# Row maxima that ignore NaN: the tiles from 53 on divided anew, shared ScalarE steps, and rows without a number found in two steps instead of three

## The chip, the cores and the metric

The kernel runs on one core of a Trainium2 chip. The time is the device time of one execution in microseconds (us). It was measured in several rounds in which the kernel before and the kernel under test ran on the same chip. The span in a profile is about 1.8 us shorter than the time of the same execution.

## The reference

```python
batch, seq, dim = 32, 2048, 2048
x = np.random.randn(batch, seq, dim).astype(np.float32)
x[np.random.rand(batch, seq, dim) < 0.1] = np.nan
np.nanmax(x, axis=-1).astype(np.float32)
```

65,536 rows of 2048 numbers, 537 MB, give 65,536 maxima. Every tenth number is a NaN and must be ignored. A row of NaN alone must give NaN. No such row occurs in the data, so the path for it was executed but never put to a test.

## The kernel before

Each of the 128 partitions takes 512 rows. They come in 74 tiles, most of 28 quarter-rows (7 rows, 7.34 MB over all partitions), into three buffers in turn. A tile is described by three lists in quarter-rows: its loads, the pieces in which it is cleaned, and its reductions.

```python
    + [([28], [7, 9, 12], [16, 12])] * 12
    + [([15, 13], [12, 12, -4], [12, 8, 8])]
    ...
    + [([4, 4, 4, 3, 5, 4, 4], [4, 4, 4, -3, 2, 3, 4, 4], [4, 4, 4, 4, 4, 4, 4])]
    + [([3, 5, 4, 1, 3, 3, 3, 2, 2, 1, 1], [-2, 1, 2, 3, 4, -1, 3, 3, -1, 2, 2, 2, -2], [4, 4, 4, 4, 4, 2, 2, 4])]
GROUPS = [TILES[:14]] + [TILES[i : i + 12] for i in range(14, 62, 12)] + [TILES[62:72], TILES[72:]]
FLAGGED = (4, 5, 6)
```

A piece passes three engines. ScalarE (ACT) turns the upper halves of its numbers into keys in which a NaN is the smallest. GpSimd (POOL), or ScalarE itself for a piece with a minus sign, turns the keys back and writes them over the numbers. VectorE (DVE) then reduces whole rows with max.

```python
e = act(here + kold, out=kp, in_=xp.bitcast(i16)[:, 1::2], func=ACT.Prelu, ...)
if back:
    e = act([e], out=xp.bitcast(i16)[:, 1::2], in_=kp, func=ACT.Copy, ...)
else:
    e = pool([e], out=xp.bitcast(i16)[:, 1::2], in0=kp, scalar1=-1.0, ...)
...
e = dve([e for a, b, e in clean if b > lo and a < done] + part, nc.vector.tensor_reduce, out=to, ...)
```

After each group named in FLAGGED, two VectorE instructions, called a step below, go over the maxima that no earlier step has gone over: one marks rows without a number, the other turns them to NaN. There are three such steps: the first, the middle and the last. The maxima of each group are stored at the end, behind all loads. A load waits for its buffer, which the last reduction of the tile three earlier frees.

## Time and profile before

| | before |
|---|---|
| time | 1254.44 us (1254.4 to 1254.58, 3 runs) |
| span in the profile | 1252.5 us |
| busy | GpSimd 93%, VectorE 89%, ScalarE 79% |
| landing of a whole tile | every 16.91 us (434 GB/s) |
| last load lands | 1242.8 us |
| last VectorE instruction ends | 1249.84 us |
| last store, 7 KB, issue to landing | 1.40 us |

The last store in the view of DMA issues (size of one, then us from issue to landing):

```profile
out_dram<-acc SPq DMA_DIRECT2D x1, 7.0 KB, 1.4
```

### The profile page before, as it was taken

What the parts mean: (1) busy time and instruction counts of PE and PEld (TensorE: products, weight loads), DVE (VectorE), ACT (ScalarE), POOL (GpSimd) and SP (SyncE); (2) the same over time, 40 slices, a digit from 0 to 9 for tenths busy, and PEclk for the clock granted to TensorE, in tenths of its full rate; (3) what the DMA queues carried; (4) which work ended last, traced back from release to release, by engine and by line L of the source; (5) the groups of instructions that cost most, each with busy time, mean ns of one, the idle gap of its engine ahead of it and who ended that gap; (6) DMA issues with size and microseconds to landing.
All of it is one profiled execution on the core that took longest, in us unless ns stands there. A gap on an engine that the chain in (4) does not pass through costs nothing.

```text
span 1252.5 us, 882 instructions
## 1 busy us (share of the span) xinstructions
DVE 1110.9 (89%) x180; ACT 987.4 (79%) x273; POOL 1168.2 (93%) x237
## 2 busy tenths in 40 slices
DVE  0888989888889988898988888898888899999999
ACT  3777887778787877788777877887777878889997
POOL 2999989998999899998999899989999999999997
DMA  9999999999999999999999999999999999999996
GB/s 414 440 418 432 440 440 440 434 416 440 440 440 436 414 440 440 438 436 425 430 440 440 438 434 418 440 440 438 436 419 436 440 426 436 429 430 434 430 427 279
DMA packets 16712, 537.20 MB, mean 429 GB/s; under 512 B 2753, under 2 KB 2753, under 8 KB 4161
## 3 DMA queue, kind: packets, MB, share of 16 engines
q1 hardware_dynamic: 16704, 537.14, 99.3%
q14 instruction: 8, 0.06, 0.0%
HBM read 536.87 MB, written 0.26 MB: 429 GB/s over the span
## 4 chain that ended last, share of the span: by engine, by line
DMA 36%; DVE 32%; POOL 21%; ACT 10%; issue 1%; SPq 0%
DMA xt<-in_x_dram 36%; DVE acc L183 32%; POOL xt L179 21%; ACT kt L175 9%; ACT xt L175 1%; DVE xt L183 0%; DVE none L183 0%; SPq L217 0%; SPq L370 0%; SPq L171 0%
## 5 line engine op out<-in xcount | busy, mean ns | idle before, releaser
L179 POOL TENSOR_SCALAR xt<-kt 128x4608 int16<-128x4608 uint16 (+10 forms) x233 | 1168.0, 5013 | 77.2 <-ACT kt L175 58.6
L183 DVE TENSOR_REDUCE acc<-xt 128x3 f32<-128x6144 f32 (+4 forms) x172 | 1107.7, 6491 | 137.7 <-POOL xt L179 128.1
L175 ACT ACTIVATE kt<-xt,scalars 128x3584 uint16<-128x3584 int16 (+8 forms) x252 | 936.8, 3755 | 256.8 <-DMA xt<-in_x_dram 233.7
L175 ACT ACTIVATE xt<-kt 128x3584 int16<-128x3584 uint16 (+5 forms) x19 | 51.2, 2697 | 0.6
L175 ACT ACT_TABLE_LOAD x1 | 1.3, 1283 | 0.9 <-SPq L171 0.9
L183 DVE TENSOR_REDUCE xt<-xt 128x1 f32<-128x1024 f32 x1 | 1.2, 1217 | 0.0
L183 DVE TENSOR_SCALAR none<-acc 128x428 int32<-128x428 f32 (+2 forms) x3 | 1.0, 339 | 0.1
L183 DVE TENSOR_TENSOR acc<-acc,none 128x428 int32<-128x428 int32 (+2 forms) x3 | 1.0, 333 | 0.1
L185 DVE MEMSET scalars<- 128x1 f32 x1 | 0.1, 59 | 1.0 <-SPq L171 1.0
L356 POOL MEMSET const-float32-0.0<- 128x1 f32 x1 | 0.1, 99 | 0.2 <-issue 0.2
L175 ACT ACTIVATE scalars<-scalars 128x1 f32<-128x1 f32 x1 | 0.2, 203 | 0.0
L356 POOL MEMSET const-bfloat16-1.0<- 128x1 bf16 x1 | 0.1, 103 | 0.0
L356 POOL MEMSET const-uint8-127<- 128x1 uint8 x1 | 0.1, 103 | 0.0
L356 POOL MEMSET const-float32-1.0<- 128x1 f32 x1 | 0.1, 99 | 0.0
## 6 DMA issues: line engine op xcount, KB each, us to landing
xt<-in_x_dram SPq DMA_DIRECT2D x60, 7168.0 KB, 22.5
xt<-in_x_dram SPq DMA_DIRECT2D x3, 3840.0 KB, 14.7
xt<-in_x_dram SPq DMA_DIRECT2D x3, 3328.0 KB, 22.2
xt<-in_x_dram SPq DMA_DIRECT2D x8, 1024.0 KB, 26.5
xt<-in_x_dram SPq DMA_DIRECT2D x2, 4096.0 KB, 21.8
xt<-in_x_dram SPq DMA_DIRECT2D x2, 3584.0 KB, 20.0
xt<-in_x_dram SPq DMA_DIRECT2D x2, 3072.0 KB, 20.6
xt<-in_x_dram SPq DMA_DIRECT2D x3, 2048.0 KB, 30.3
```

The lines of the kernel that those rows point to most:

```text
L175: return order.add("act", nc.scalar, lambda: nc.scalar.activation(**kw), deps)
L179: "pool", nc.gpsimd, lambda: nc.gpsimd.tensor_scalar(**kw), deps
L183: return order.add("dve", nc.vector, lambda: do(**kw), deps)
L185: e_top = order.add("dve", nc.vector, lambda: nc.vector.memset(top, EDGE), [])
L356: nc = _bacc.Bacc("TRN2", target_bir_lowering=False, num_devices=1)
```

## The change

The intent is to bring VectorE's end nearer to the last landing. Three things change: the tiles from 53 on are divided differently, with fewer reductions (164 for 173); neighbouring pieces may share one ScalarE key step (a tuple in the list); and groups and steps are placed so that the first step over the maxima falls before the last fourteen tiles and the second at the very end.

```diff
-    + [([28], [7, 9, 12], [16, 12])] * 12
-    + [([15, 13], [12, 12, -4], [12, 8, 8])]
...
+    + [([19, 9], [12, (5, -7), 4], [12, 16])]
...
+    + [([6, 5, 4, 5, 4, 4], [6, 5, (-3, 1), 3, 2, 4, (-2, 2)], [4, 8, 8, 8])]
+    + [([5, 4, 4, 4, 3, 4, 4], [2, 3, 4, (1, -2), 2, 3, 3, 4, (-1, 3)], [4, 8, 4, 4, 4, 4])]
+    + [([4, 4, 3, 2, 3, 4, 1, 2, 3, 2], [4, 4, 3, -2, 3, (3, -1), 3, (-1, 1), 2, -1], [4, 4, 4, 4, 4, 4, 4])]
...
-GROUPS = [TILES[:14]] + [TILES[i : i + 12] for i in range(14, 62, 12)] + [TILES[62:72], TILES[72:]]
-FLAGGED = (4, 5, 6)
+GROUPS = [TILES[i : i + 15] for i in range(0, 60, 15)] + [TILES[60:]]
+FLAGGED = (3, 4)
...
-                for c in pieces:
-                    back, c = c < 0, abs(c) * Q
+                for parts in pieces:
+                    parts = parts if isinstance(parts, tuple) else (parts,)
+                    c = sum(map(abs, parts)) * Q
...
+                    for c in parts:
+                        back, c = c < 0, abs(c) * Q
```

## The prediction

> **What bounds the kernel now.** I read the page's DMA rows first, because a kernel that reads 537 MB and writes almost nothing may have nothing else to gain.
>
> ```profile
> DVE 1110.9 (89%) x180; ACT 987.4 (79%) x273; POOL 1168.2 (93%) x237
> ...
> DMA  9999999999999999999999999999999999999996
> GB/s 414 440 418 432 440 440 440 434 416 440 440 440 436 414 440 440 438 436 425 430 440 440 438 434 418 440 440 438 436 419 436 440 426 436 429 430 434 430 427 279
> ```
>
> The DMA row has 9 in every slice but the last. Counting active packets in the trace, at least one DMA engine was idle in only about 1 us between 2 us and 1242 us. So the loads run without a hole, and only the last slice holds idle time. The landing events tell the same: a whole tile (28 quarter-rows in each partition, 7.34 MB) lands every 16.91 us (434 GB/s), and the last load lands at 1242.8. The change reads the same bytes, so that moment is a floor. From there to the span's end at 1252.5 lie 9.7 us, and 1.2 us of that is the ending that follows the last store.
>
> Second, the chain of waits in order of time, from 1000 us on:
>
> ```profile
> 998.68 22.52 DMA xt<-in_x_dram
> ...
> 1021.22 3.29 ACT kt L175
> ...
> 1119.85 7.05 POOL xt L179
> ...
> 1126.92 14.70 DVE acc L183 x3
> ...
> 1142.05 33.88 DVE acc L183 x8
> ...
> 1247.15 2.29 DVE acc L183
> ...
> 1249.67 0.17 DVE acc L183
> ```
>
> A load lands at 1021.20 (tile 60, counting from 0), then 21 ACT and POOL steps follow without a hole, and from 1126.92 VectorE works through to 1249.84. The end is therefore not set by the last load but by a backlog: VectorE is some 28 us behind the loads in the middle of the program and needs the last fourteen tiles to catch up. The end is **the start of that VectorE run plus everything VectorE still has to do**.
>
> Third, the groups of instructions by shape give durations, which scatter by under 1%:
>
> ```profile
> L183 DVE TENSOR_REDUCE acc<-xt 128x4 f32<-128x8192 f32 x56 | 486.4, 8687 | 118.9 <-POOL xt L179 118.7
> L183 DVE TENSOR_REDUCE acc<-xt 128x3 f32<-128x6144 f32 x61 | 399.1, 6543 | 0.1
> ...
> L183 DVE TENSOR_REDUCE acc<-xt 128x1 f32<-128x2048 f32 x22 | 48.8, 2279 | 9.2 <-POOL xt L179 9.2
> ...
> L183 DVE TENSOR_SCALAR none<-acc 128x428 int32<-128x428 f32 x1 | 0.6, 607 | 0.0
> ...
> L183 DVE TENSOR_SCALAR none<-acc 128x70 int32<-128x70 f32 x1 | 0.2, 234 | 0.0
> ```
>
> A row costs (8687 - 2279)/3 = 2136 ns, one reduction 2279 - 2136 = 143 ns on top. In the run the next reduction starts 83 ns before the last one ends, so an instruction saved is worth about **0.06 us**, not 0.14. The 118.9 us of idle time before reductions of 8192 is no loss: it lies in the middle of the program, where the loads bound.
>
> **What the Trainium skill says.** "DMA: Bandwidth & Descriptors", section Bandwidth, gives a ceiling of 435 GB/s from 16 ports; the trace has 434, so no cutting of loads can speed them up. Its section "Latency and other measured facts" warns that a row pitch at a large power of two slows transfers; the new groups change the pitch (105 rows of 8 KiB for 84), but the groups of before with 92, 84, 70 and 14 rows all run at the rate one formula gives (0.03 us a load plus its bytes), so I expect nothing from it. "VectorE: DVE Perf Modes", the perf-mode tier table, has tensor_reduce at 1x only[...]. Its section on the TRN2 errata says that each instruction pays a fixed extra time, so that many small tiles cost more than one large; the 143 ns above agree.
>
> **The change part by part.**
>
> Loads: 108 for 109, and 0.03 us each. Nothing. The last landing stays at about 1242.5.
>
> Start of the run. I rebuilt the order of instructions with what each waits for, and added measured durations step by step: an instruction starts when its engine is free and its inputs are there (ACT 0.09 us before the previous ends, POOL 0.08 after it, 0.03 after a wait, 0.08 from ACT to POOL). As a check, before's chain from 1021.20: ACT 3.28, POOL 4.20, ACT 5.42, POOL 7.04 + 7.04, ACT 1.99 + 2.49 + 3.28, POOL 4.20, ACT 5.42, POOL 7.04 + 5.34 + 4.20 + 4.77 + 7.04 + 6.48 + 3.05 + 7.04, ACT 2.84 + 5.42, POOL 7.04. With the gaps that gives 1126.81; the trace has 1126.92. In the changed kernel the chain starts a tile later, with tile 61's landing at 1021.20 + 16.91 = 1038.11: ACT 3.28, POOL 4.20, ACT 5.42 three times, the copy back on ACT of 7 quarters 4.20, ACT 1.99 + 3.69, POOL 4.77, ACT 5.42, POOL 7.04 + 7.04 + 3.05 + 3.63 + 3.63 + 4.77 + 6.48. VectorE then starts the second reduction of tile 65 (4 rows, 8.69) at 1117.99, and tile 66 at 1126.58; with the 0.11 by which the check was short, about **1126.7**, against 1126.92: a gain of 0.2.
>
> Work of the run, tiles 66 to 73, the same 56 rows in both:
> - Reductions: 38 before, 33 after: 5 x 0.063 = 0.32 saved.
> - The middle step for rows without a number (70 columns, two instructions) lay inside the run, between the reduction that ends at 1217.99 and the one that starts at 1218.44: 0.45 and the lost overlap of 0.08, 0.53 saved. The first step (now 414 columns) moves to 1033, where VectorE still waits some 1.8 us a tile: free.
> - The last step covers 98 columns for 14: (607 - 234)/358 = 1.04 ns a column, two instructions: 0.17 lost.
> - The row reduced in two halves, the second waiting for the first (1245.97 to 1246.01): 0.12 saved.
> Sum -0.80, so 122.92 becomes 122.1, and VectorE ends at 1126.7 + 122.1 = **1248.8** for 1249.84.
>
> Store: the last one has 392 B a partition for 56. The eight packets of a DMA engine took 11 ns each at 56 B and 22 ns at 368 B: 0.1 lost. It took 1.40 us from issue to landing.
>
> Shared ScalarE steps: each saves about 0.3 us of ACT time. ACT is not the bound in the run, so this has no term of its own; it counts only by keeping the run fed.
>
> Sum: -0.2 - 0.8 + 0.1 = -0.9, so 1254.44 - 0.9 = 1253.5.
>
> **The rivals.**
> 1. VectorE runs dry near the end. In my addition the least lead of a cleaned piece over the reduction that needs it is 0.04 us in tile 69, 0.07 in tile 71 and 0.43 at the last row, and VectorE will be 0.1 to 0.2 earlier than added up there. The last rows hang on landings, so a delayed load goes straight into the end. For it: three landings of before were late by 0.4, 0.6 and 0.2 us, each with an 8 KB instruction fetch on the DMA queue, and stayed late. Against it: the leads of the last tile are 0.3 to 0.6. It would take half the gain: 1254.0. I put 0.1 of it into the prediction.
> 2. The loads are disturbed: a new pitch, or a queue that runs empty since buffers come free at other times. 1% would be 12 us: 1266. Against it: loads of before were issued 14 us and more ahead of landing, and none of my added-up issues came too late.
> 3. A large gain because ACT and POOL are freed: impossible past the floor. If every engine were idle at 1242.5, one ACT step of 512 (0.71), its way back (0.77), a row (2.28), two small steps (0.5), store and ending (1.4 + 1.2) end at 1249.4, 3 us under now: 1251.4.
>
> **Range and chances.** The centre is -0.9, with 0.1 for rival 1: **1253.6 us**. Executions of before lie within 0.2 us, late landings move both kernels by up to about 0.5, and rival 1 can eat the gain: 8 in 10 between **1253.0** and **1254.5**. A 2% step is 25 us, more than twice all the time between the last landing and the end, so faster by 2% is as good as impossible (0.005); slower by 2% would need rival 2 (0.01); the same 0.985.
>
> **What would show it.** Right: a DMA row unchanged; the final unbroken VectorE run in the chain starts near 1118.0 instead of 1126.9, with 34 reductions; its middle holds no step on "none", the first of which sits near 1033 and the second has 98 columns; it ends near 1248.8. Wrong: gaps before reductions in tiles 66 to 73, released by POOL or ACT; tiles landing further apart than 16.91 us; a last load clearly after 1242.8; a last store above 1.6 us.

## The result, and the profile after

The changed kernel took 1253.89 us in the median of six runs (1253.55 to 1254.31), the kernel before 1254.42 (1254.28 to 1254.58) beside it. The ratio is 0.9996 with a 95% interval of 0.9983 to 1.0009: the same within 2%.

The page of the changed kernel, its rows of busy time and of transfers:

```profile
DVE 1110.5 (89%) x169; ACT 988.5 (79%) x271; POOL 1166.9 (93%) x239
...
DMA  9999999999999999999999999999999999999997
GB/s 415 440 421 429 440 440 440 424 427 440 440 440 427 424 440 440 438 431 421 440 440 438 432 420 440 440 438 434 418 440 440 436 438 421 431 434 426 430 427 289
```

The transfers are what they were, a 9 in every slice but the last. The last load lands at 1242.7. The chain of waits of the changed kernel in order of time, from 1000 us on (start, us, what):

```profile
1016.18 21.75 DMA xt<-in_x_dram
...
1037.96 3.29 ACT kt L186
...
1045.59 5.34 POOL xt L190
...
1050.96 66.86 DVE acc L194 x9
...
1117.88 23.30 DVE acc L194 x4
...
1193.46 10.93 DVE acc L194 x3
1204.38 0.01 issue
1204.39 0.02 DVEq L124
1204.41 0.04 issue
1204.45 8.27 DVE acc L194 x2
...
1245.93 2.30 DVE acc L194
...
1248.55 0.26 DVE acc L194
```

Where the chain of before still had GpSimd and ScalarE up to 1126.9, it has VectorE from 1050.96 on. The restart that the prediction put at 1117.99 is there, at 1117.88. From tile 66 on (1126.48) only two reductions start late, one in tile 71 (at 1204.45) by 0.16 us and the last (at 1245.93) by 0.04. Late is counted against the usual overlap: the next reduction otherwise starts 0.08 before the last one ends. The last instruction ends at 1248.81, and the prediction said 1248.8. The steps over the maxima, among the groups by shape:

```profile
L194 DVE TENSOR_SCALAR none<-acc 128x414 int32<-128x414 f32 x1 | 0.6, 593 | 0.0
L194 DVE TENSOR_TENSOR acc<-acc,none 128x414 int32<-128x414 int32 x1 | 0.6, 587 | 0.0
L194 DVE TENSOR_SCALAR none<-acc 128x98 int32<-128x98 f32 x1 | 0.3, 264 | 0.0
L194 DVE TENSOR_TENSOR acc<-acc,none 128x98 int32<-128x98 int32 x1 | 0.3, 257 | 0.0
```

And the last store in the view of DMA issues of the changed kernel:

```profile
out_dram<-acc SPq DMA_DIRECT2D x1, 49.0 KB, 1.7
```

To compare profiles whose loads landed at slightly different times, I use one number in the rest: **VectorE's end counted from the landing of tile 61**, the tile whose landing starts the last unbroken stretch of the changed kernel (before's starts with tile 60, whose landing is 16.91 us earlier). Before it is 1249.84 - 1038.11 = 211.72 us (from unrounded times), after it is 1248.81 - 1037.93 = 210.87: a gain of 0.85.

### The profile page after: what moved, and what is told of

Read it like the earlier page. It is cut to its first block, busy times and chain, and to the rows that moved or that the text cites. A ratio compares the mean times of both kernels' runs of the same rounds, so it can differ in the third digit from the quotient of the medians. Undisturbed runs are those within 1.5% of the kernel's fastest.

```text
span 1251.8 us, 872 instructions
## 1 busy us (share of the span) xinstructions
DVE 1110.5 (89%) x169; ACT 988.5 (79%) x271; POOL 1166.9 (93%) x239
## 4 chain that ended last, share of the span: by engine, by line
DVE 37%; DMA 35%; POOL 17%; ACT 10%; issue 1%; SPq 0%; DVEq 0%
DVE acc L194 37%; DMA xt<-in_x_dram 35%; POOL xt L190 17%; ACT kt L186 9%; ACT xt L186 1%; SPq L228 0%; DVE none L194 0%; DVEq L124 0%; SPq L384 0%; SPq L182 0%
## 5 line engine op out<-in xcount | busy, mean ns | idle before, releaser
L190 POOL TENSOR_SCALAR xt<-kt 128x3584 int16<-128x3584 uint16 (+8 forms) x235 | 1166.7, 4965 | 78.7 <-ACT kt L186 60.1
L186 ACT ACTIVATE kt<-xt,scalars 128x3584 uint16<-128x3584 int16 (+9 forms) x248 | 936.0, 3812 | 255.8 <-DMA xt<-in_x_dram 237.9
L186 ACT ACTIVATE xt<-kt 128x3584 int16<-128x3584 uint16 (+4 forms) x21 | 53.5, 2545 | 0.7
```

The lines of the kernel that those rows point to most:

```text
L186: return order.add("act", nc.scalar, lambda: nc.scalar.activation(**kw), deps)
L190: "pool", nc.gpsimd, lambda: nc.gpsimd.tensor_scalar(**kw), deps
```

## The experiments

Twelve runs were made on three chips (e1 to e4, e5 to e8, e9 to e12). All were correct. "Change to before" is the difference of medians. Kernels are compared only within the same rounds. The last two columns are of the one profiled execution of each.

| run | median, us | change to before | VectorE's end after tile 61 landed | last store, issue to landing |
|---|---|---|---|---|
| before | 1254.42 | | 211.72 | 1.40 |
| changed | 1253.89 | -0.53 | 210.87 | 1.66 |
| e1 regroup only | 1254.15 | -0.16 | 211.31 | 1.53 |
| e2 tiles only | 1254.63 | +0.32 | 212.06 | 1.40 |
| e3 unshared | 1254.56 | +0.25 | 211.32 | 1.69 |
| e4 changed again | 1253.71 | -0.60 | 210.82 | 1.72 |
| e5 GpSimd step | 1253.50 | -1.11 | 210.63 | 1.54 |
| e6 two last stores | 1254.38 | -0.23 | 210.86 | 2.05 |
| e7 unshare tile 62 | 1254.15 | -0.46 | 210.87 | 2.15 |
| e8 middle step | 1253.84 | -0.77 | 211.15 | 1.40 |
| e9 changed, third | 1254.01 | -0.50 | 210.88 | 1.69 |
| e10 GpSimd step again | 1253.69 | -0.82 | 210.62 | 1.55 |
| e11 middle step, wide store | 1254.37 | -0.14 | 211.26 | 1.71 |
| e12 middle step again | 1253.93 | -0.58 | 211.24 | 1.40 |

The second and third profile of the changed kernel (e4, e9) show that the number is steady: 210.87, 210.82, 210.88. Of before, e1, e2 and e3 there is one profile each. Every run against before is "same", since the 95% intervals are about 1.6 us to either side. What follows rests on the profiles and medians.

### e1: the new groups alone

```diff
-GROUPS = [TILES[:14]] + [TILES[i : i + 12] for i in range(14, 62, 12)] + [TILES[62:72], TILES[72:]]
-FLAGGED = (4, 5, 6)
+GROUPS = [TILES[i : i + 15] for i in range(0, 60, 15)] + [TILES[60:]]
+FLAGGED = (3, 4)
```

> The kernel before with its old tiles, but with the new groups (15 tiles each, two steps for rows without a number). My theory (the end is the start of the last unbroken VectorE run plus the work in it): the run still starts at tile 66 near 1126.9, the middle step of 0.53 us is gone from it, the last step covers 98 columns and costs 0.17 more, so VectorE ends at 1249.84 - 0.36 = 1249.5; with the larger last store (1.66 us for 1.40 in the changed kernel) about 1254.3 in all, 0.1 us under before. Rival A (the two-step part is the whole gain): VectorE ends at 1248.8 and the time is 1253.9.

VectorE's end came 0.41 us earlier, 0.36 was expected, and the time fell by 0.16, 0.1 was expected. Of the 0.41, tile 66 started 0.06 earlier and the work from there took 0.35 less, so the middle step was in the run and cost what its two instructions and the lost overlap say. Part of the gain went to the larger store (1.53 us for 1.40). Rival A falls: regrouping is not the whole gain. Tiles landed every 16.9 us with groups of 105 rows too, so the new row pitch costs nothing.

### e2: the new tiles alone

```diff
-GROUPS = [TILES[i : i + 15] for i in range(0, 60, 15)] + [TILES[60:]]
-FLAGGED = (3, 4)
+GROUPS = [TILES[:14]] + [TILES[i : i + 12] for i in range(14, 62, 12)] + [TILES[62:72], TILES[72:]]
+FLAGGED = (4, 5, 6)
```

> The changed kernel with its new tiles and shared steps, but with the old groups and three steps for rows without a number. My theory: not a gain but a loss. The new tiles leave VectorE no idle time from tile 61 on, so that the first step (428 columns, 1.2 us), which before fell into a hole, now lies in the run, and the middle step too: VectorE ends near 1250.4 (1249.8 before, 1248.8 changed), time about 1255.0. Rival A (parts add up, tiles bring what regrouping does not): VectorE ends at about 1249.3, time about 1253.9.

A loss, as expected, though smaller: VectorE's end came 0.34 us later than before (0.6 was expected), the time rose by 0.32. The chain of waits of e2 shows the first step inside the stretch:

```profile
1051.43 15.16 DVE acc L194 x2
...
1066.61 0.62 DVE none L194
...
1067.25 51.09 DVE acc L194 x8
```

In the kernel before, this step ran from 1064.54 to 1065.78 and the next reduction then still waited for GpSimd until 1065.91; it cost nothing. With the new tiles VectorE has no hole there. Counted from the changed kernel (210.87), 1.6 us was expected and 1.19 came, because a later VectorE no longer meets late pieces: neither those that hold the changed kernel up by 0.23 us in tiles 64 and 65, nor those that cost it 0.20 from tile 66 on. In e2 no reduction from tile 62 on is late. So the two parts do not add up: -0.41 alone and +0.34 alone make -0.85 together. The tiles are worth something only once the first step is out of their way.

### e3: no shared ScalarE steps

```diff
-    + [([19, 9], [12, (5, -7), 4], [12, 16])]
+    + [([19, 9], [12, 5, -7, 4], [12, 16])]
(and the seven other tuples taken apart in the same way)
```

> The changed kernel with every shared ScalarE step taken apart into one step a piece (eight more ScalarE steps, same pieces, same loads). What I predicted of the change: the sharing has no term of its own, so VectorE ends at 1248.8 as in the changed kernel. Theory after working it through step by step: ACT lies in the chain that feeds the run (tile 62), so tile 66 starts about 0.2 us later, and VectorE waits for ACT pieces near the end: VectorE ends near 1249.2, time 0.4 us above the changed kernel.

VectorE's end came 0.45 us later than in the changed kernel (0.4 expected). Tile 66 started 0.17 later, and reductions of tiles 70 and 71 started late by 0.10 and 0.36. The chain of e3 shows why those were late, ScalarE and then GpSimd between landing and reduction:

```profile
1157.30 25.99 DMA xt<-in_x_dram
...
1183.31 3.08 ACT kt L186
...
1188.09 1.92 ACT xt L186
1190.02 1.43 ACT kt L186
1191.44 0.07 issue
1191.51 1.90 POOL xt L190
```

So the sharing has a term of its own, which the prediction had denied. The median lay 0.85 above e4, more than the profile explains; the scatter of e3 was the widest of all (1254.32 to 1255.45), and what made its slow runs slow is open.

### e4 and e9: the changed kernel again

No edit.

> The changed kernel again, beside the others on the same chip, for a second profile. Its six runs so far spread over 0.76 us, those of before over 0.30, and the one profile was of the fastest. Theory (rival 1 of the prediction: the shortened end has little lead over the landings, so late landings now reach the end): a profile of a slower run shows a gap before one of the last reductions, released by ACT or POOL that waited for a load, or a start of the run later than 1126.5 by the delay of tile 61's landing. Rival (the store): VectorE ends at 1248.8 again and the last store takes longer than 1.66 us. Median 1253.9, spread again 0.5 or more.

> The changed kernel, to stand beside the next three on one chip. Theory (the wide last store of 392 B a partition is what scatters: 1.53 to 2.15 us in five profiles, against 1.40 in each of four profiles with 56 B): VectorE ends 210.8 to 210.9 us after tile 61's landing, the store takes 1.5 to 2.2 us; median 0.5 to 0.6 us under before, scatter over 0.5 us. Rival (the scatter is only that of the landings): the store takes 1.66 again and the scatter is as wide in all four kernels.

Of e4's theory one half came true: no new gap stands before the last reductions, but the run starts later by the delay of tile 61's landing. The store as the cause, e9's theory, fails for the profiled executions: it took 1.66 to 1.72 us in all three. Their spans were 1251.78, 1252.70 and 1252.34, and tile 61 landed at 1037.93, 1038.85 and 1038.47. The differences are the same (0.92 and 0.56 in the spans, 0.92 and 0.54 in the landings). A late landing far from the end shifts the whole rest. In e4 the packets of 57,344 B took longer than 2.2 us 64 times, 58 of them between 30 and 133 us, where the first profile has none; each of the landings that they delayed stayed late. What slowed them is not in the trace. In e9 it was tiles 15 and 56 that landed later, by 0.44 and 0.41, and tile 26 earlier by 0.40, each after one of the instruction reads told of in the last section. The unprofiled runs of e9 fall into two heaps, 1253.6 and 1254.0 to 1254.1; without profiles their cause stays open. So does why the changed kernel scattered over 0.54 us there and the three beside it over only 0.19 to 0.23.

### e7: only the shared step of tile 62 taken apart

```diff
-    + [([19, 9], [12, (5, -7), 4], [12, 16])]
+    + [([19, 9], [12, 5, -7, 4], [12, 16])]
```

> The changed kernel with only the shared ScalarE step of tile 62 taken apart (12 and (5,-7) and 4 become 12, 5, -7, 4). Theory: this step is in the chain that feeds the run, so tile 66 starts 0.17 us later after tile 61's landing (88.55 in the changed kernel, 88.72 with all steps taken apart), and VectorE ends 0.1 to 0.2 later (its later small waits take up a part); time +0.15. Rival (only the shared steps of the last tiles count, where ACT alternates with GpSimd): tile 66 starts at 88.55 and VectorE ends as in the changed kernel.

Half of each came true. Tile 66 started 0.18 us later (88.73 after tile 61's landing), as the theory said. But VectorE ended as in the changed kernel, 210.87, as the rival said: the later VectorE found the pieces of tile 71 ready, and the 0.20 of late starts shrank to 0.01. The last 0.18 of the earlier start is therefore worth nothing in the changed kernel, since the late tiles set the end along with it. What the sharing brings in e3 comes from the last tiles.

### e8 and e12: a middle step put back

```diff
-GROUPS = [TILES[i : i + 15] for i in range(0, 60, 15)] + [TILES[60:]]
-FLAGGED = (3, 4)
+GROUPS = [TILES[i : i + 15] for i in range(0, 60, 15)] + [TILES[60:72], TILES[72:]]
+FLAGGED = (3, 4, 5)
```

> The changed kernel with a third step for rows without a number put back after tile 71 (84 columns), the last one with 14 columns as before. Theory: the step costs its two instructions and the lost overlap, 0.57 us, in a run without holes; later waits (0.04 at the last row) and the shorter last step (-0.17) leave VectorE's end 0.4 later (211.25 us after tile 61's landing), and the smaller last store (-0.26) leaves 0.13 us in the time. Rival (the step hides in waits of the run): VectorE's end 0.17 earlier.

> The version with the middle step and a last store of 14 columns (56 B a partition), again. Theory: VectorE ends 211.15 us after tile 61's landing, the store takes 1.40 us; median 0.5 to 0.8 us under before, as good as the changed kernel or better although VectorE ends 0.3 us later; scatter 0.3 us. Rival (store size does not matter): 0.3 us above the changed kernel.

VectorE's end came 0.28 and 0.37 us later than in the changed kernel (0.4 expected), yet the time was no worse: in the call with e9 it was 0.08 lower. The last store is what paid most of it back, 1.40 us for 7 KB in both.

### e11: the same, with one wide store

```diff
 GROUPS = [TILES[i : i + 15] for i in range(0, 60, 15)] + [TILES[60:]]
 FLAGGED = (3, 4)
+MIDDLE = 72
...
+                if number == MIDDLE:
+                    e_mid = step(accs[:, flagged : first + base // D], ...)
+                    flagged = first + base // D
```

> The version with the middle step put back after tile 71, but with one store of 98 columns (392 B a partition) at the end instead of an early one of 84 and a last one of 14. It differs from the next kernel in the store alone. Theory: VectorE ends 211.15 us after tile 61's landing as there; the store takes 1.5 to 2.2 us for 1.40, so the median is 0.25 to 0.5 us above the next kernel's and the scatter is wider. Rival: same time, same scatter.

This isolates the store: the VectorE work and its end (211.26 and 211.24) are those of e12. The median is 0.44 us higher, and the store took 0.31 longer in the profile. The lines of e11, then of e12:

```profile
out_dram<-acc SPq DMA_DIRECT2D x1, 49.0 KB, 1.7
```

```profile
out_dram<-acc SPq DMA_DIRECT2D x1, 42.0 KB, 11.9
out_dram<-acc SPq DMA_DIRECT2D x1, 7.0 KB, 1.4
```

The 42 KB of e12 leave early, behind the loads, and land 5 us before VectorE ends. The part of the theory on scatter falls: e11 scattered over 0.19 us, e12 over 0.21. In this pair the wide store is slower, not less steady, though over all profiles its time varies more (see the table: 1.53 to 2.15 us for 49 KB, 1.40 each time for 7 KB).

### e6: two stores after the last step

```diff
-GROUPS = [TILES[i : i + 15] for i in range(0, 60, 15)] + [TILES[60:]]
-FLAGGED = (3, 4)
+GROUPS = [TILES[i : i + 15] for i in range(0, 60, 15)] + [TILES[60:73], TILES[73:]]
+FLAGGED = (3, 5)
```

> The changed kernel with its last group cut in 91 and 7 columns, one step for both, so that two stores are issued after the step instead of one. Theory: VectorE's end stays (210.85 us after tile 61's landing); the second, small store is issued 0.45 us later and takes 1.40 us, so the end comes 0.2 us later than with the single store of 1.66 us. Rival (the count of stores costs nothing, their size does): the end comes 0.26 us earlier.

The direction was right, the size was not: from VectorE's end to the landing of the second store it took 2.45 us, with the one store of the changed kernel 1.69. The second store was issued 0.38 after the first and took 2.05, not 1.40. In this one profile a small store right behind another took longer than a lone one. Splitting helped in e5, e10 and e12, where the other part went at least 1.7 us earlier.

### e5 and e10: GpSimd takes over most of the last step

```diff
-GROUPS = [TILES[i : i + 15] for i in range(0, 60, 15)] + [TILES[60:]]
-FLAGGED = (3, 4)
+GROUPS = [TILES[i : i + 15] for i in range(0, 60, 15)] + [TILES[60:73], TILES[73:]]
+FLAGGED = (3, 5)
+ON_POOL = 4
...
+                e = order.add("pool", nc.gpsimd, lambda: nc.gpsimd.tensor_scalar(
+                    out=mark, in0=mine, scalar1=NONE, scalar2=float(0x00800000),
+                    op0=ALU.is_equal, op1=ALU.mult), waits)
+                e = order.add("pool", nc.gpsimd, lambda: nc.gpsimd.tensor_tensor(
+                    out=mine.bitcast(i32), in0=mine.bitcast(i32), in1=mark, op=ALU.add), [e])
```

The mark is added to the bits instead of or-ed to them. The correct results show that this add leaves the bits of ordinary maxima whole. For a row without a number, 0xFF7F0000 + 0x00800000 is meant to give the same NaN bits as the OR did; the data have no such row, so that was not seen.

> An attempt to beat the changed kernel. The last step for rows without a number is cut in two: the 91 columns of tiles 60 to 72 are done by GpSimd, which is idle from about 1245.8 while VectorE still reduces, and stored at once; VectorE does the 7 columns of the last tile alone. Theory: GpSimd does its two instructions by 1246.7, so that nothing waits for them; VectorE's last step costs 0.33 us for 0.52 (-0.19), the last store has 28 B a partition and takes about 1.40 us for 1.66 (-0.26): 0.45 us under the changed kernel, about 1253.4, with VectorE's end 210.65 to 210.7 us after the landing of tile 61 (210.85 changed). Rival: GpSimd's two small instructions take over 1 us or slow VectorE's last reduction, and nothing is gained.

> The version with GpSimd's share of the last step again, now beside the changed kernel. Theory: VectorE ends 210.65 us after tile 61's landing, the last store of 28 B a partition takes 1.4 to 1.55 us; median 0.4 to 0.5 us under the changed kernel in the same rounds. Rival (the lower time in its first call was the chip's or chance): within 0.1 us of the changed kernel.

VectorE's end came 0.24 and 0.26 us earlier than in the changed kernel, and the last store took 1.54 and 1.55 for 1.66 to 1.72. That is not the 1.40 expected: with 28 B a partition it took longer than the lone stores of 56 B, so less is not always faster. Beside the changed kernel (e9) the median was 0.32 us lower, 0.4 to 0.5 was expected; against before it is -1.11 and -0.82. The timeline of e5 shows the two GpSimd instructions beside VectorE's last reductions (start, us, engine):

```profile
1243.88 4.53 DVE L196 TENSOR_REDUCE acc<-xt 128x1 f32<-128x2048 f32 x2
...
1246.10 0.55 POOL L332 TENSOR_SCALAR mark<-acc 128x91 int32<-128x91 f32 x1
1246.73 0.34 POOL L345 TENSOR_TENSOR acc<-acc,mark 128x91 int32<-128x91 int32 x1
1247.10 2.07 SPq L381 DMA_DIRECT2D out_dram<-acc  x2
1248.44 0.17 DVE L196 TENSOR_SCALAR none<-acc 128x7 int32<-128x7 f32 x1
```

They took 0.89 us together, with no sign of slowing VectorE, and the store of 91 columns was on its way 1.74 us before the last. This version has the lowest medians of all, though 1 us of 1254 stays far within the 2% of "same".

## Why the prediction was right, and where its steps were off

**The bound.** Right. Transfers to the last landing, then a VectorE backlog; the rows of transfers did not change, and nearly all of the difference between the three changed profiles lies in their landings. The forecast "the same within 2%" tests little: all that lies behind the last landing is under 1% of the time. What tests the account is its sum.

**Start of the run.** Right in place: 88.55 us after tile 61's landing, predicted 1126.7 - 1038.11 = 88.6. But e7 shows that delaying it by 0.18 changes nothing at the end, so most of the 0.2 that the sum credits to it is not a gain that stands alone.

**Work of the run.** Predicted 122.1, measured 122.32. The items were right: from tile 66 on, e1 took 0.35 less than before (the two items of regrouping, -0.53 and +0.17), and e2 0.43 less (the other two, fewer reductions and the row in halves, -0.32 and -0.12). What was missing is 0.20 of late starts in tiles 71 and 73. This is rival 1 in a small form, for which I had set aside 0.1. Its predicted path through late landings was not what the profiles show: the late starts come to 0.14 to 0.20 us in three profiles with landings up to 0.92 us apart, and the landings after tile 61's follow it at the same distance within 0.1 us up to tile 72. So they seem to come from the division of the tiles itself; no run tests that alone.

**Store.** This is the term that was mis-sized. Predicted 0.1 from the packets alone. The store took 0.26 to 0.32 us longer in the three profiles of the changed kernel, and e11 against e12 shows 0.44 in the median. The trace splits it: from issue to the end of the last packet it is 1.04 us before and 1.15 after, the 0.1 of the prediction. What was missed lies between the last packet and the landing: 0.36 to 0.37 in the four profiles with 56 B a partition, 0.38 to 1.01 in the seven with 392 B, but 0.52 and 0.53 with the 28 B of e5 and e10 too. So size alone does not set it. Where it is over 0.38, the landing events of the 16 DMA engines show a pause of 0.12 us or more among them; what causes the pause is open.

**Shared ScalarE steps.** "No term of its own" was wrong: e3 measures 0.45 us in VectorE's end. That ACT is not the busiest engine in the run did not matter, since a single late piece stops a reduction. The total was not hurt, because the step-by-step addition had the shared steps in it.

**Sum.** Predicted -0.9 (-0.8 with the margin): -1.0 to VectorE's end and +0.1 for the store. Measured: -0.85 to VectorE's end and about +0.3 for the store make -0.55, and the medians say -0.53, -0.60 and -0.50. The 1253.89 lies in the range, 0.3 above the centre, by the store and the 0.2 of late starts.

**Rivals 2 and 3.** No disturbance of the loads by the new pitch or by late issues: tiles still land every 16.9 us. The floor was not approached.

## What to carry to other kernels

When a stream of loads runs without a hole, count what lies behind its last landing before tuning anything: here it was 9.7 us of 1254, and all that newly divided tiles could win was part of it. In such a tail the gain of one part depends on the holes that the other parts leave, so test parts alone and together, and compare profiles from a common landing, since landings alone moved by 0.9 us between executions. Send what is ready early, so that a small store is left for the end (56 B a partition landed soonest here, 28 B did not beat it), and let idle engines take what can be done before the last result.

## What the Trainium skill lacked or had wrong

- "DMA: Bandwidth & Descriptors" (Specifications) tells of slower transfers below 512 B, but no page gives the measured latency of a small store from the sync engine's queue by its size. Here a lone one of 56 B a partition took 1.40 us from issue to landing in four profiles, one of 392 B 1.53 to 2.15 us in seven and one of 28 B 1.54 and 1.55 in two; a store of 28 B issued 0.38 us behind another took 2.05.
- The same page (Queues, rings and completion order) names a runtime-internal queue row but not what its traffic costs a full stream. Between 200 us and the end, each profile of before and of the changed kernel has seven reads of 8 KB on the instruction queue; five of the seven coincide with a packet of 57,344 B that took 0.2 to 0.5 us longer than the usual 2.12, and after three of these a tile (15, 26 and 56) landed 0.15 to 0.70 us late and stayed so.

On the fixed cost of a VectorE instruction nothing was lacking. "VectorE: DVE Perf Modes" (the TRN2 errata) gives two fixed terms, 58 cycles and, as measured for a single instruction, about 150. At the page's 0.96 GHz they are, by my estimate, 60 and 156 ns. The runs agree with both: a reduction has 143 ns of its own, but in an unbroken row the next one starts 83 ns before the last ends, so that one fewer saves 0.06 us.
